# A state-space scan in chunks of 8 tokens and two halves of the groups instead of chunks of 4 and four quads, with its taps written through DRAM

## The chip, the cores and the metric

The kernel runs on one core of a Trainium2 chip. The core has five engines with a queue of instructions each: PE (TensorE) for matrix products, DVE (VectorE), ACT (ScalarE) and POOL (GpSimd) for elementwise work, and SP (SyncE), which here does nothing but issue the transfers (DMAs). The metric is the time of one execution in microseconds; the median of several runs counts.

## The reference

It is one decoder layer on 512 tokens of width 1024, in float32. A modulated RMS norm of x goes through one input projection, whose columns feed two groups of heads: a state-space mixer (S5) and a sparse attention. Both are gated, joined, projected and added to x. The change is in the state-space mixer. It has 32 groups of 16 channels, each with a complex diagonal state of 64 (`a_re`, `a_im`):

```python
lam_bar = jnp.exp(lam * dt)
b_bar = ((lam_bar - 1.0) / lam)[..., None] * b_mat
bu = jnp.einsum('gpc,bsgc->bsgp', b_bar, ug)
_, states = lax.associative_scan(_ssm_combine, (a_seq, bu), axis=1)   # s_t = lam_bar * s_(t-1) + bu_t
y = jnp.einsum('gcp,bsgp->bsgc', c_mat, states).real + d_skip * uf
z = jax.nn.gelu(y)
z = z * jax.nn.sigmoid(z @ w_glu + b_glu)
```

The attention scores each pair of tokens with an indexer, keeps the 128 best keys of each query, and takes a softmax over them with a bias that depends on the distance (`rel_bias`, by buckets).

## The kernel before

**Recording and order.** The kernel's functions don't issue instructions. They record them in `P`, stage by stage, with the engines that each may run on. `Plan.schedule` then simulates the five engines with the costs of `_cost`, and sets the order on every engine by the numbers of the tables STAGES (a start and a slope for each stage), SHIFT (an offset for a name in a stage), ONLY (the engines allowed), SLOTS (buffers of each pool) and KEEP. `_paired` says which instructions of DVE and POOL the planner lets wait for one another. `Plan.issue` puts the result out, so every instruction of the program has one line, L422. The order on an engine is fixed when the program is built; at run time an engine takes the next instruction as soon as what it needs is there, and what stands behind a waiting instruction waits too. All DMAs stand in SP's one queue.

**The work, in the order of its stages.** x0, x1: the norm of the two halves of x; x is transposed on PE (px). mod0 to mod4: the modulation's products (pm, pmt) and, as each piece of 128 channels of h comes (split into a high and a low part, hh and hl), the products of the index projection (pi), whose inputs are 640 columns of `in_w_in`. Every projection is three products for one (hh with wh, hl with wh, hh with wl), because the weight `wr` is split into `wh` and `wl` by ACT, DVE or POOL. Then come the values v0 and v1 (pv, pt), the index scores and the top keys (pr, acc, MAX8, MATCH_REPLACE8), the gates za, z2, z3 and the queries and keys qk0 to qk3 (all pp), the attention in four pairs of heads (pl, lg, ppt, po, at0 to at3), the gated linear unit of the state-space part (pgl, glu) and the output projection (pout).

**The state-space part.** `tables(q)` makes, for each quad q of 8 groups, what the scan needs: the weights W1 that take 4 tokens into the state (padded to 32 rows for the pairs of groups: padw, made by `cprod`, transposed by PE as ptw), W2 that takes the state back (w2, five powers of the decay), the taps Kt (pK, the direct way from inputs to outputs inside a chunk) and the block-triangular T, which is cleared by a memset on POOL and filled by four DMAs from kd, a copy of Kt in DRAM. `ssm_quad(q)` does the scan itself. The inputs u of one quad lie in U as 128 rows (4 tokens x 32) by 4 x 128 chunks. pd is W1 times U; DVE turns it by the phase (cos, sin), scans with the decay (TENSOR_TENSOR_SCAN) and turns it back (Xr, Xi); py is T times U plus W2 times Xr and Xi. Its result goes through a gelu and, through yd in DRAM, back to channel order (zt). U comes through DRAM too (ud).

**The bias.** `bias_rows` writes a row of biases for each of the 8 heads to bd in DRAM, and one DMA from DRAM to DRAM repeats it 128 times into bskew, from which each attention tile reads its skewed bias G.

Of the kernel before, what the change touches and what calls it, by code (L numbers as in the profile page):

```python
# [111 lines left out]
def _cost(eng, method, args, kw):  # L112
# [17 lines left out]
    if eng == "DVE":  # L130
# [7 lines left out]
        if method in ("tensor_copy", "tensor_scalar", "tensor_scalar_mul") and not ps:  # L138
            return 80 + 61 * aps + 0.521 * n
        return 69 + 61 * aps + 1.042 * n  # L140
# [18 lines left out]
def _paired(eng, method, args, kw):  # L159

    if eng == "POOL":
        return method not in ("memset", "iota")
# [10 lines left out]
    return n >= 2  # L173


class Plan:
# [73 lines left out]
    def schedule(self):  # L250
# [48 lines left out]
        while len(order) < len(ops):  # L299
# [68 lines left out]
            if e == "SP":  # L368
# [4 lines left out]
                dma = max(dma, hw + 500) + size / 305.0 * (2 if v.shape[-1] < 128 else 1)  # L373
                fin = dma + 900
# [50 lines left out]
class Eng:  # L425
# [18 lines left out]
SLOTS = {"t2": 65, "raw": 4, "ws": 8, "w2": 4, "psum": 8, "m8": 8}  # L444
BYTES = {"t2": 2048, "raw": 4096, "ws": 4096, "w2": 2560, "m8": 32}
KEEP = {"t2": 0, "raw": 15, "ws": 9, "w2": 0, "psum": 0, "m8": 0}
WINDOW = 506.5
# [7 lines left out]
    "const": (-753.2, 27.26), "warm": (-173.12, 802761090585146.2), "x0": (-752.23, 136.21), "x1": (-422.14, 15.05),  # L455
    "half0": (-64.92, 331.47), "half1": (108.73, 2.354074717163716e+16), "cond": (-674.9, 21.09),
    "cols": (-477.52, 211.29), "pars": (-269.91, 1.06), "mod0": (-469.03, 178.39), "mod1": (-148.91, 4.96),
    "mod2": (-149.72, 4.8), "mod3": (-159.94, 81.59), "mod4": (-64.92, 2.52), "idx2": (-240.13, 67.24),
    "idx": (66.28, 1.52), "rel": (-97.06, 84.25), "par": (123.19, 7.61), "lam": (-133.39, 1.1441577559218786e+16),
# [131 lines left out]
def record(P, a, out):  # L591
# [394 lines left out]
    def cprod(Xr, Xi, q, nd, nm, dst, neg):  # L986
# [8 lines left out]
        for e in range(2):  # L995
            G.memset(dst[e], 0.0)
# [564 lines left out]
```

## Time and profile before

| | |
|---|---|
| median of 3 runs | 358.12 us (356.9, 358.93, 358.12) |
| profiled execution | 355.87 us |
| its span, first to last instruction | 354.2 us |
| PE busy | 324.9 us, 92% |
| DVE busy | 289.4 us, 82% |
| ACT, POOL busy | 129.9 us, 110.5 us |
| PE's mean granted clock | 0.964 |

The span leaves out 1.67 us of the execution around the first and last instruction. Busy time says how long an engine had an instruction in it. An engine at 92% can still be the one that sets the end, and what matters then is what it waits for in the remaining 8%, and whether its products run at its full clock (1.0 is 2.4 GHz, and the lower level is half).

### The profile page before, as it was taken

Reading aid. Unit: us, or ns where it says so; the run is one execution under the profiler, and the core shown is the slowest. Engines: PE = TensorE matmul, PEld = TensorE weight load, DVE = VectorE, ACT = ScalarE, POOL = GpSimd, SP = SyncE. Lnnn points to the kernel's source line nnn. Section 1 sums busy time; section 2 is a strip of 40 time slices with the busy share of each in tenths; the row PEclk is TensorE's granted clock in tenths of the full one; section 3 lists DMA queues with packets and bytes.
Section 4 is the critical chain, followed back from the end, with each engine's and each line's share of the span. In section 5 each row is a group of like instructions: output and inputs, shape, how many; then the busy total and the mean of one; then the engine's idle time right before and its main releaser. Section 6 shows DMA issues by size and latency. Waiting matters only on the chain.

```text
span 354.2 us, 5839 instructions
## 1 busy us (share of the span) xinstructions
PE 324.9 (92%) x2022; PEld 265.4 (75%) x2023; DVE 289.4 (82%) x679; ACT 129.9 (37%) x264; POOL 110.5 (31%) x143
## 2 busy tenths in 40 slices
PE   5829969999995997999999998999999999999996
PEld 3717649788783886888888867877888777888785
DVE  5677994889999199999994999999999795896613
ACT  3423452117472116533431152332555884303000
POOL 3740227031974926531542600201800201100000
PEclk9879978999999699999999999999999999999999
DMA  7799775724264221623714483461380107266011
GB/s 224 221 307 348 139 227 160 214 62 118 52 192 144 82 62 49 187 64 116 207 34 119 127 237 104 138 210 40 93 269 28 59 3 268 89 216 230 30 61 60
DMA packets 57358, 49.50 MB, mean 140 GB/s; under 512 B 11224, under 2 KB 47400, under 8 KB 57328
## 3 DMA queue, kind: packets, MB, share of 16 engines
q1 hardware_dynamic: 57328, 49.13, 46.7%
q8 instruction: 16, 0.26, 0.3%
q14 instruction: 14, 0.11, 0.1%
HBM read 44.64 MB, written 6.05 MB: 143 GB/s over the span
## 4 chain that ended last, share of the span: by engine, by line
PE 67%; DVE 16%; DMA 10%; SPq 3%; issue 2%; ACT 1%; POOL 0%; DVEq 0%; POOLq 0%; ACTq 0%
PE pp L422 24%; PE pout L422 11%; PE pi L422 5%; PE pl L422 4%; DMA bskew<-bd 4%; PE pt L422 3%; PE py L422 3%; PE pgl L422 3%; PE po L422 3%; SPq L422 3%; PE ppt L422 2%; PE pv L422 2%; DVE stg L422 2%; PE pd L422 2%; DMA wa<-in_w_ada_dram 2%
## 5 line engine op out<-in xcount | busy, mean ns | idle before, releaser
L422 PE MATMUL pp<-hh,wh 128*128 128x512 f32 x152 | 61.5, 406 | 4.4 <-POOL wh L422 4.4
L422 PE MATMUL pp<-hl,wh 128*128 128x512 f32 x152 | 60.7, 400 | 0.0
L422 PE MATMUL pp<-hh,wl 128*128 128x512 f32 x152 | 60.2, 403 | 0.0
L422 POOL TENSOR_TENSOR wl<-wr,wh 128x1024 fp32r<-128x1024 f32 (+1 forms) x15 | 35.6, 2385 | 37.7 <-ACT wh L422 24.0
L422 ACT ACTIVATE wh<-wr 128x1024 fp32r<-128x1024 f32 (+1 forms) x27 | 25.9, 971 | 34.6 <-PE pout L422 20.5
L422 PEld LDWEIGHTS pp<-hh,wh 128*128 128x128 f32 x152 | 29.3, 193 | 10.4 <-POOL wh L422 4.8
L422 PEld LDWEIGHTS pp<-hl,wh 128*128 128x128 f32 x152 | 29.3, 193 | 5.7
L422 PEld LDWEIGHTS pp<-hh,wl 128*128 128x128 f32 x152 | 29.0, 191 | 6.0 <-issue 0.4
L422 DVE TENSOR_TENSOR wl<-wr,wh 128x1024 fp32r<-128x1024 f32 (+1 forms) x24 | 27.3, 1156 | 7.5 <-PE pi L422 4.6
L422 PE MATMUL pout<-wl,yh 128*128 128x512 f32 (+1 forms) x72 | 26.4, 367 | 0.4 <-DVE wl L422 0.4
L422 PE MATMUL pout<-wh,yl 128*128 128x512 f32 (+1 forms) x72 | 26.1, 366 | 0.0
L422 PE MATMUL pout<-wh,yh 128*128 128x512 f32 (+1 forms) x72 | 26.0, 370 | 0.1
L422 DVE MATCH_REPLACE8 work<-m,work 128x256 f32<-128x256 f32 (+2 forms) x45 | 24.1, 539 | 0.0
L422 DVE MAX8 m<-work 128x8 f32<-128x256 f32 (+2 forms) x45 | 23.2, 545 | 0.0
L422 ACT ACTIVATE lg<-lg,nm 128x256 f32<-128x256 f32 (+3 forms) x32 | 17.6, 552 | 4.1 <-DVE nm L422 4.1
L422 DVE TENSOR_TENSOR pout<-pout,gb 128x512 f32<-128x512 f32 (+1 forms) x9 | 5.7, 638 | 15.1 <-PE pout L422 15.0
L422 PE MATMUL pi<-hh,wh 128*128 128x384 f32 (+2 forms) x50 | 15.8, 361 | 1.6 <-DVE hh L422 1.6
L422 DVE CUSTOM_DVE_ANT_0 lg<-pl,G 128x256 f32<-128x256 f32 (+3 forms) x32 | 13.8, 485 | 3.4 <-PE pl L422 3.4
L422 POOL TENSOR_SCALAR wh<-wr 128x1024 fp32r<-128x1024 f32 x9 | 9.7, 1083 | 21.6 <-PE pp L422 13.2
L422 PE MATMUL pi<-hl,wh 128*128 128x384 f32 (+2 forms) x50 | 16.2, 338 | 0.0
L422 PE MATMUL pi<-hh,wl 128*128 128x384 f32 (+2 forms) x50 | 15.9, 339 | 0.0
L422 PEld LDWEIGHTS pout<-wl,yh 128*128 128x128 f32 x72 | 13.6, 189 | 2.8 <-DVE wl L422 0.6
(292 smaller groups left out, 792.2 us busy)
## 6 DMA issues: line engine op xcount, KB each, us to landing
wa<-in_w_ada_dram SPq DMA_DIRECT2D x32, 256.0 KB, 5.8
wr<-in_w_in_dram SPq DMA_DIRECT2D x13, 512.0 KB, 4.6
wr<-in_w_in_dram SPq DMA_DIRECT2D x24, 256.0 KB, 3.3
wr<-in_w_out_dram SPq DMA_DIRECT2D x8, 512.0 KB, 5.7
wag<-in_w_ada_dram SPq DMA_DIRECT2D x8, 512.0 KB, 5.0
x<-in_x_dram SPq DMA_DIRECT2D x8, 256.0 KB, 3.6
xr<-in_x_dram SPq DMA_DIRECT2D x8, 256.0 KB, 5.4
out_dram<-oo SPq DMA_DIRECT2D x7, 256.0 KB, 3.8
```

What stands on the lines that cost most here:

```text
L422: getattr(engines[eng], method)(*[val(a) for a in args], **{k: val(a) for k, a in kw.items()})
```

## The change

The scan works on 8 tokens a chunk, so a row of U holds 8 tokens x 16 channels and there are 64 chunks instead of 128. Instead of four quads there are two halves of the groups, each of two quads' tables: `ssm_half(r)` runs after tables 1 and 3. The two quads of a half lie in the upper and lower 64 partitions of the state, and share one chain of DVE instructions. Their pd products have 64 stationary columns each and are issued in pairs, side by side; the products with the states have 64 rows each and are paired too. The weights W1 and W2 have no zeros to be filled in any more. The taps with their zeros go to a DRAM tile zd, 256 x 240, and each T tile is read from it by 8 strided DMAs of 64 KB (before: 4 DMAs of 16 to 64 KB into a cleared tile). U is read by one DMA of 256 KB per quad. bskew is four tiles of two heads. Parameters are loaded in more and smaller pieces. Buffer counts change (t2 from 65 to 52, and a new pool tt of 6), the planner treats POOL's memsets as excluding DVE's paired operations, and gives DRAM writes a longer latency; and all numbers of the order are new, so that every engine's order differs. In the profile of the changed kernel the line of all instructions is L431.

```diff
 def _paired(eng, method, args, kw):
     if eng == "POOL":
-        return method not in ("memset", "iota")
+        return True
...
-SLOTS = {"t2": 65, "raw": 4, "ws": 8, "w2": 4, "psum": 8, "m8": 8}
+SLOTS = {"t2": 52, "tt": 6, "raw": 4, "ws": 8, "w2": 4, "psum": 8, "m8": 8}
...
-    "tab3": (287.71, 23.67), "u0": (42.98, 31.6), "u1": (57.28, 511.21), "ssm0": (304.54, 320.39),
+    "tab3": (-371.6824, 65.9471), "u0": (269.1514, 95.3904), "u1": (352.9992, 4.1434), "ssm0": (785.1089, 222.22),
...
-    Q = (128, 4, 128)
+    Q = (128, 8, 64)
...
-        for e in range(2):
-            G.memset(dst[e], 0.0)
...
-        Tt = t2(f"T{q}", shape=Q, parts=True)
-        G.memset(Tt, 0.0)
-        kd_ = P.tile("dram", f"kd{q}", [128, 128])
-        N.dma_start(kd_, Kt)
-        for jj in range(4):
-            N.dma_start(Tt[32 * jj:32 * jj + 32, :, (3 - jj) * 32:128],
-                        kd_[:, 0:(jj + 1) * 32].rearrange("(m c) x -> c m x", m=4))
+        N.dma_start(ZD[r][128 * (q % 2):128 * (q % 2) + 128], Kt)
+        if q % 2:
+            for h in range(2):
+                Tt = TT[2 * r + h] = P.tile("tt", f"T{2 * r + h}", [128, 8, 128], parts=True)
+                for i in range(8):
+                    N.dma_start(Tt[i::8], ZD[r].raw((16, 8, 128), lambda t, i=i, h=h: bass.AP(
+                        tensor=t.tensor, offset=t.offset + 16 * h * 240 + (7 - i) * 16,
+                        ap=[[240, 16], [32 * 240, 8], [1, 128]])))
...
-    def ssm_quad(q):
+    def ssm_half(r):
...
-            for m in range(4):
-                T.matmul(pd[:, m * 128:(m + 1) * 128], W1[q, e][:, m * 128:(m + 1) * 128], U[:, m, :],
-                         start=True, stop=True)
+            for m in range(8):
+                with P.together():
+                    for h in range(2):
+                        T.matmul(pd[64 * h:64 * h + 64, m * 64:(m + 1) * 64], W1[r][e][:, m, 64 * h:64 * h + 64],
+                                 Us[h][:, m, :], start=True, stop=True, skip_group_check=True)
...
+        for m in range(8):
+            o = slice(m * 64, m * 64 + 64)
+            for h in range(2):
+                T.matmul(pys[h][:, o], TT[2 * r + h][:, m], Us[h][:, m],
+                         start=(m == 0), stop=False, skip_group_check=True)
+        for m in range(8):
+            o = slice(m * 64, m * 64 + 64)
+            for e, x_ in enumerate((Xr, Xi)):
+                with P.together():
+                    for h in range(2):
+                        p_ = slice(64 * h, 64 * h + 64)
+                        T.matmul(pys[h][:, o], W2[2 * r + m // 4][e][p_, m % 4, 1:9].rearrange("p d c -> p (d c)"),
+                                 x_[p_, m], start=False, stop=(e == 1 and m == 7), skip_group_check=True)
...
-        N.dma_start(bskew.rearrange("h (p n) -> h p n", n=385)[:, :, 0:384],
-                    bd.raw((8, 128, 384), lambda t: bass.AP(tensor=t.tensor, offset=t.offset + 256,
-                                                            ap=[[640, 8], [0, 128], [1, 384]])))
+        for i in range(4):
+            bskew.append(P.tile("dram", f"bskew{i}", [2, 128 * 385]))
+            N.dma_start(bskew[i].rearrange("h (p n) -> h p n", n=385)[:, :, 0:384],
+                        bd.raw((2, 128, 384), lambda t, i=i: bass.AP(tensor=t.tensor, offset=t.offset + 1280 * i + 256,
+                                                                     ap=[[640, 2], [0, 128], [1, 384]])))
```

The order at three places. First, POOL in the norm of x, before (x is scaled by rstd; w, T, bb, padw, Xr and Xi are buffers of the tables):

```order
L422 TENSOR_SCALAR x_1_68<-x_1_68,rstd_40_201 128x512
L422 TENSOR_SCALAR x_4_74<-x_4_74,rstd_40_201 128x512
L422 MEMSET Xi_246 128x4
L422 MEMSET padw_53_249 128x512
L422 MEMSET Xr_253 128x4
L422 TENSOR_TENSOR wl_276<-wr_170,wh_259 128x640
L422 MEMSET w_11_65_305 128x640
L422 MEMSET T_70_327 128x512
L422 MEMSET w_01_73_341 128x640
L422 MEMSET bb_75_355 128x128
L422 MEMSET bb_77_362 128x128
L422 MEMSET padw_79_368 128x512
```

and with the change:

```order
L431 MEMSET bb_45_179 128x128
L431 MEMSET Kt_182 128x112
L431 MEMSET blk_115 64x1 x4
L431 TENSOR_SCALAR x_6_78<-x_6_78,rstd_56_226 128x512
L431 TENSOR_TENSOR wl_317<-wr_186,wh_298 128x640
L431 TENSOR_SCALAR x_12_90<-x_12_90,rstd_73_320 128x512
L431 TENSOR_SCALAR hf_485<-xT_65_278,Ac_105_462,Bc_102_456 128x256
L431 TENSOR_SCALAR wh_501<-wr_376 128x640
```

The clearing of padw, w and T that stood among and behind the scalings of x is gone, and what memsets there are stand ahead of them.

Second, the queue of transfers (SP) at the bias table, before:

```order
L422 DMA kd_330_1346<-Kt_1330 128x128
L422 DMA wr_338_1363<-in_w_in_dram 128x4x128 x2
L422 DMA bskew_1369<-bd_933 1024x1x384
L422 DMA T_97_433<-kd_327_1338 32x4x32
L422 DMA T_97_433<-kd_327_1338 32x4x64
L422 DMA T_97_433<-kd_327_1338 32x4x96
L422 DMA T_97_433<-kd_327_1338 32x4x128
L422 DMA T_70_327<-kd_330_1346 32x4x32
L422 DMA T_70_327<-kd_330_1346 32x4x64
L422 DMA T_70_327<-kd_330_1346 32x4x96
L422 DMA T_70_327<-kd_330_1346 32x4x128
L422 DMA wr_365_1495<-in_w_in_dram 128x4x128 x2
```

and with the change:

```order
L431 DMA ud_251_1050<-us_1042 128x512
L431 DMA bskew_253_1055<-bd_913 256x1x384
L431 DMA bskew_254_1057<-bd_913 256x1x384
L431 DMA bskew_256_1062<-bd_913 256x1x384
L431 DMA bskew_258_1067<-bd_913 256x1x384
L431 DMA G_259_1070<-bd_913 128x256
L431 DMA G_260_1074<-bd_913 128x256
L431 DMA U_1110<-ud_251_1050 128x8x64
L431 DMA wr_273_1127<-in_w_in_dram 128x4x256
L431 DMA wr_275_1143<-in_w_in_dram 128x4x256
```

The T loads that stood behind bskew, in front of the next weight (wr) and ud, are gone from there; four smaller transfers are followed by G, U and weights.

Third, PE at the last scan. Before, between the taps' products of one quad (py_2513) and those of the last (py_2565):

```order
L422 MATMUL py_2513<-Xi_566,w_13_493_2068 128x128
L422 MATMUL prt_2534<-ident_70,rp_1617 128x128 x4
L422 MATMUL pp_2492<-hh_187_734,wh_555_2376 128x512
L422 MATMUL pp_2492<-hl_190_748,wh_555_2376 128x512
L422 MATMUL pp_2492<-hh_187_734,wl_563_2408 128x512
L422 MATMUL pp_2492<-hh_185_726,wh_555_2376 128x512
L422 MATMUL pp_2492<-hl_197_775,wh_555_2376 128x512
L422 MATMUL pp_2492<-hh_185_726,wl_563_2408 128x512
```

and so on, twelve weight products pp in all, up to `py_2565<-U_1217,T_141_564`. With the change, behind the last pd product (pd_2735) of the second half to run:

```order
L431 MATMUL pd_2735<-U_1814,w_10_542_2556 64x64
L431 MATMUL pn_2766<-ident_86,nsq_2724 128x128 x4
L431 MATMUL psel_2773<-ident_86,blk_579_2713 128x128 x2
L431 MATMUL py_2798<-U_1814,T_586_2754 128x64 x8
L431 MATMUL prt_2815<-ident_86,rp_2150 128x128 x4
L431 MATMUL py_2821<-U_1110,T_592_2782 128x64 x8
L431 MATMUL pbx_2835<-rT_2823,sel_2826 128x512
L431 MATMUL pbx_2837<-rT_2823,sel_2826 128x512
L431 MATMUL pbx_2840<-rT_2823,sel_2826 128x512
L431 MATMUL pbx_2842<-rT_2823,sel_2826 128x512
L431 MATMUL py_2821<-Xr_2675,w_00_534_2513 128x64
L431 MATMUL py_2798<-Xr_2675,w_00_534_2513 128x64
```

Between the last pd and the first product with Xr stand transposes of the norm, the T products and four pbx, and no weight product.

## Rows read from the trace of the kernel before

**Rows 1.** The page: busy time, share and instructions of each engine.
```profile
PE 324.9 (92%) x2022; PEld 265.4 (75%) x2023; DVE 289.4 (82%) x679; ACT 129.9 (37%) x264; POOL 110.5 (31%) x143
```

**Rows 2.** Windows: span, busy us (instructions), PE's clock, DMA share, GB/s.
```profile
0.00:31.60 31.60, 19.87 (x186) 14.53 (x186) 20.31 (x63) 12.54 (x25) 14.05 (x54) 0.84 0.88 266
31.60:50.80 19.20, 16.07 (x123) 11.65 (x123) 17.70 (x76) 7.66 (x14) 5.36 (x2) 0.95 0.84 213
50.80:63.50 12.70, 12.68 (x59) 11.89 (x63) 7.87 (x20) 3.39 (x6) 6.41 (x8) 0.81 0.55 162
...
114.30:124.30 10.00, 10.00 (x42) 8.42 (x43) 2.68 (x7) 1.11 (x3) 9.54 (x11) 0.69 0.28 80
...
200.00:222.00 22.00, 19.89 (x139) 15.41 (x138) 20.82 (x41) 9.52 (x14) 1.92 (x1) 1.00 0.60 171
222.00:306.00 84.00, 83.29 (x609) 67.64 (x609) 74.66 (x189) 43.24 (x105) 18.79 (x14) 1.00 0.38 121
```

**Rows 3.** Chain that ended last, at the start: start us, us, what.
```profile
14.31 7.47 DVE stg L422
```

**Rows 4.** Timeline, 14 to 24 us: start us, us, engine, line, operation.
```profile
14.45 0.64 POOL L422 MEMSET w<- 128x640 f32 x1
14.66 0.19 ACT L422 ACTIVATION_READ_ACCUMULATOR junk<-x 128x1 f32 x1
...
21.69 0.15 POOL L422 MEMSET Xr<- 128x4 f32 x1
21.82 0.16 DVE L422 TENSOR_TENSOR ms<-ss 128x2 f32<-128x2 f32 x1
```

**Rows 5.** POOL's instructions by line and shape: count, busy us, mean ns.
```profile
L422 POOL MEMSET w<- 128x640 f32 x8 | 4.9, 636 | 4.8 <-PE py L422 4.8
```

**Rows 6.** Chain that ended last, 95 to 114 us.
```profile
95.97 12.84 DMA bskew<-bd
...
113.20 1.06 POOL wh L422
```

**Rows 7.** Timeline, 96 to 115 us, DMA queue and PE.
```profile
96.78 12.34 SPq L422 DMA_DIRECT2D T<-kd  x8
...
114.30 0.80 PE L422 MATMUL pp<-hh,wh 128*128 128x512 f32 x1 [4.35 <-POOL wh L422]
```

**Rows 8.** Chain that ended last, four runs of PE records.
```profile
122.23 1.79 PE pd L422 x16
...
218.31 2.92 PE py L422 x24
...
255.85 3.23 PE pt L422 x27
...
292.64 4.52 PE po L422 x80
```

**Rows 9.** Timeline, PE at 280 us.
```profile
280.44 0.72 PE L422 MATMUL pl<-qk,qk 64*128 64x128 f32 x8
```

**Rows 10.** DVE's instructions by line: count, busy us, mean ns.
```profile
L422 DVE TENSOR_TENSOR pd<-pd,cos 128x512 f32<-128x512 f32 x16 | 10.6, 689 | 0.0
...
L422 DVE TENSOR_TENSOR_SCAN pd<-dec,pd 128x512 f32<-128x512 f32 x8 | 9.4, 1206 | 0.0
...
L422 DVE CUSTOM_DVE_ANT_0 lg<-pl,G 128x256 f32<-128x256 f32 (+3 forms) x32 | 13.8, 485 | 3.4 <-PE pl L422 3.4
```

**Rows 11.** Chain that ended last, 212 to 219 us.
```profile
212.96 1.92 DMA kd<-Kt
...
216.21 1.91 DMA T<-kd
```

**Rows 12.** Timeline, 214 to 219 us, DMA queue and PE.
```profile
214.90 1.74 SPq L422 DMA_DIRECT2D T<-kd  x4
...
218.31 0.46 PE L422 MATMUL py<-U,T 128*128 128x128 f32 x2 [1.26 <-DMA T<-kd]
```

More of the change, by code (lines that the diff above doesn't have):

```diff
@@ L139, in _cost @@
             return 80 + 61 * aps + 0.521 * n
+        if out.base.name in ("ya", "ys") and len(out.shape) > 2:
+            return 69 + 1.94 * n
         return 69 + 61 * aps + 1.042 * n
@@ L173, in _paired, with _dram @@
     return n >= 2
+def _dram(way):
+    vs = [isinstance(v, View) and v.base.pool == "dram" for v in way[2][:2]]
+    return vs[0], all(vs)
 class Plan:
@@ L553 @@
-    "bias:pb": -124.7, "bias:brow": 18.6, "bias:brow2": -6.1, "bias:bd": 26.1, "bias:bskew": -26.1,
[18 rows of a table removed]
+    "const:ident": 85.268, "const:identb": 22.023, "const:zero": 40.092, "warm:pi0": -41.874, "warm:pi1": 32.785,
[4 rows of a table added]
+    "cols:psm": 3.997, "cols:mcol": -1.031, "pars:ld2": -40.116, "pars:stg": -15.44, "pars:pst": 6.806,
[19 rows of a table added]
+    "par:blk": -49.228, "par:blk4": 9.999, "par:psel": -35.233, "par:sel": 99.294, "par:hpi": -22.367,
+    "par:nrow": -43.414, "par:ones_n": -1.15, "par:ones_f": -9.762, "lam:st1": 81.265, "lam:st2": -20.414,
[5 rows of a table added]
@@ new lines @@
+    "bc:c_re_l": -6.972, "bc:cd": 9.033, "bc:pcm": 3.882, "bc:c_re_t": 2.04, "bc:c_im_t": 0.998,
[29 rows of a table added]
+    "norm:pn": 24.679, "norm:rq_s": 23.609, "norm:rqk": 67.517, "norm:rq_t": 1.602, "norm:rp": 27.307,
+    "norm:prt": -1.164, "norm:rT": -8.38, "bias:rbp": -10.194, "bias:oh": -9.493, "bias:oh_r": 4.246,
+    "bias:pb": 2.666, "bias:brow": 4.148, "bias:brow2": 30.786, "bias:bd": -47.516, "bias:bskew0": 31.287,
[16 rows of a table added]
+    "gate:wag": -1.883, "gate:pmg": 9.221, "gate:grow_h": 62.367, "gate:pgb": 1.642, "gate:gb0": 1.092,
@@ L572 @@
+    "gate:gb1": 23.929, "out0:wl2": -0.966, "out0:xr": -73.998, "out0:oo": 80.526, "out0:out": 3.708,
+    "out1:wr2": 0.123, "out1:wh2": 7.903, "out1:wl2": -3.805, "out1:xr": 14.489, "out1:pout": -0.182,
+    "out1:oo": 0.061, "out1:out": -5.254,
 }
@@ L833, in record @@
     stage("par")
-    eye = small("eye", [128, 32], parts=True)
-    for r in range(4):
-        p_ = slice(32 * r, 32 * r + 32)
-        V.tensor_copy(eye[p_], ident[p_, p_])
+    eye4, eye2, eye = small("eye4", [128, 64]), small("eye2", [128, 32]), small("eye", [128, 16])
+    V.tensor_add(eye4, ident[:, 0:64], ident[:, 64:128])
+    V.tensor_add(eye2, eye4[:, 0:32], eye4[:, 32:64])
+    V.tensor_add(eye, eye2[:, 0:16], eye2[:, 16:32])
     causal = small("causal", [128, 128])
@@ L922, in record @@
     cmul(Pr[:, 2], Pi[:, 2], Pr[:, 1], Pi[:, 1], Pr[:, 1], Pi[:, 1], (128, 16))
[L923 to L925 removed]
+    for d in (2, 4):
+        up = lambda P_: P_[:, d:d + 1].to_broadcast([128, d, 16])
+        cmul(Pr[:, d + 1:2 * d + 1], Pi[:, d + 1:2 * d + 1], Pr[:, 1:d + 1], Pi[:, 1:d + 1], up(Pr), up(Pi), (128, d, 16))
+    nPr = st((128, 9, 16))
     V.tensor_scalar(nPr, Pr, -1.0, None, op0=ALU.mult)
[L927 to L929 removed]
+    Pr7, Pi7 = (small(nm, [128, 8, 16], parts=True) for nm in ("Pr7", "Pi7"))
+    for i in range(8):
+        hi(Pr7[:, i], Pr[:, 7 - i])
+        hi(Pi7[:, i], Pi[:, 7 - i])
+    rho8 = st()
+    V.tensor_mul(rho8, rho, rho)
+    V.tensor_mul(rho8, rho8, rho8)
+    V.tensor_mul(rho8, rho8, rho8)
     den, nr, cfr, cfi, tq = st(), st(), st(), st(), st()
@@ L1292, in norms @@
         evac(rT, prt)
-    bd, bskew = P.tile("dram", "bd", [8, 640], parts=True), P.tile("dram", "bskew", [8, 128 * 385])
+    bd, bskew = P.tile("dram", "bd", [8, 640], parts=True), []
     def bias_rows():
```

227 lines of the change are left out of this document (115 added, 112 removed), and 200 rows, old and new, of tables (ONLY, SHIFT, STAGES).

## The prediction

> **What bounds the kernel now.** I read the page first, then the windows, then the chain of work that ended last, and last the timeline at the places where the chain leaves TensorE. The page has PE at work for 324.9 of 354.2 us and DVE for 289.4 [rows 1]. So a DVE instruction that goes is worth something only where PE stands still for it, and PE's own time and its idle time have to be counted apart. I cut the windows where PE stands or runs slowly [rows 2]. It idles 11.7 us up to 31.6, where the first index projection (pi) starts, 3.1 us from there to 50.8, and 2.1 us between 200 and 222. From 114.3 to 124.3 it never idles, but its granted clock is 0.69; from 50.8 to 63.5 the clock is 0.81. From 222 to 306, the attention, PE is busy for 83.3 of 84 us and DVE for 74.7. Elsewhere there is little to win but PE's own work.
>
> At three places the kernel stands for something that the change touches. First, the chain has a DVE copy of a 16x128 tile (stg) that takes 7.47 us [rows 3]. The timeline shows what lies beside it: ACT has the last square sum of x at 14.85; POOL begins a run of memsets at 14.45 and ends it at 21.84; the copy ends at 21.78, and the norm's next DVE operation (ms) starts at 21.82 [rows 4]. I read the copy as held by the whole run. Second, the transfer that writes bskew lasts 12.84 us, and POOL's split of a weight behind it starts only at 113.20 [rows 6]. In that stretch the queue needs 12.34 us for eight issues of T tiles, and PE starts again at 114.30, after 4.35 idle us [rows 7]. Third, PE waits 1.26 us for the taps T [rows 12].
>
> **The change part by part.** *Start.* The 8 memsets of w take 4.9 us of POOL [rows 5]; with the tables' zero padding they go, those of padw and T too. In the order no run of memsets is left behind POOL's first scalings of x; the next one there comes forty rows later. If nothing holds the copy, the norm can go on at 14.9 instead of 21.82: 6.9 us. More can come back behind it, since PE's 3.1 idle us up to 50.8 and its slow clock from 50.8 to 63.5 (0.81 over 12.7 us: 2.4 us of work) are of the same wait for the modulation. Transfers set the limit: their engines are 0.88 and 0.84 busy up to 50.8 and 0.55 in the next 12.7 us [rows 2], so what comes after 63.5 can't move up by more than those 12.7, and the new kernel has more small parameter loads in front. I take -10, between the copy alone (-7) and -12; below, -0.6 is the bound.
>
> That bound is one of a page. The Trainium skill, page "SBUF — State Buffer", section "Who interferes with whom", says that DVE and GpSimd share a pair of ports under an exclusive lock, held for one whole instruction, so that the second to come waits for the other's instruction. By that, the copy would have waited for one memset (0.64 us in the row of rows 4), and the sum would be +4.5. The trace has the copy end with the last memset of the run and not with the first, and I go by the trace.
>
> *The bias table.* The transfer of bskew becomes four, of two heads each, and on the queue no T load stands behind them: there come G tiles, U and the weights of za, which PE takes only after the products of v0 and of the index scores, far later. The stall of 4.35 us goes. The 10 us behind it, at 0.69, hold 6.9 us of work at full clock, so 3.1 more go: -7.4. Bounds: 0, if the queue is held there by these four in the same way, and -7.5.
>
> *The scan's products.* A quad has 16 records of pd in 1.79 us and 24 of py in 2.92 (two records to a product) [rows 8]; four quads make 18.8 us. After the change there are 64 half-width products of pd in pairs (128 records), 32 of T (64 records) and 64 row halves on the states (128 records), all with 64 moving columns where there were 128. The trace has none with 64. Nearest to pd are the 80 records of po, column halves in pairs, in 4.52 us [rows 8], 0.057 each: 7.3. For T I take the price of the full products now, 0.117: 7.5. Nearest to the row halves are 8 records of pl with 64 rows in 0.72 us [rows 9], 0.09 each: 11.5. Together 26.3, or +7.5. If half the columns cost half, it is 13.2 (-5.6); if nothing pairs and columns don't count, 320 records at 0.117 are 37.4 (+18.6). I take +4: the prices are those of 128 columns, and some of the halving should show, most on T.
>
> *Vector work.* Two of four scan chains go: eight products of about 0.69 us, four sums like them and two scans of 1.206 each [rows 10], some 10.7 us a chain, 21 together. I count nothing for it, because PE is busy beside DVE with the projections; where that cover ends, at the last scan, the next term has it. The bound is -3. The wider tables, the powers and the small copies of Pr7 and Pi7 go the other way on DVE and ACT and are hidden alike.
>
> *The last half.* Now the taps of the last two quads and their scan end together. The order shows that behind the last pd there are left only the transposes pn, psel and prt, the taps' products and four pbx before PE needs the states; twelve weight products (pp) stood between the last two scans' products before. The taps need a write of Kt (1.92 to land), sixteen issues of 0.44 (four take 1.74), and 1.91 to land [rows 11, 12]: 10.8 us. The states need the chain of 10.7 and some 2.4 of norm operations among it: 13 us. PE has in that time 3.7 us of T products (half of the 64 records at 0.117) and about 2 of the rest: 7.3 idle, less the 2.1 of before [rows 2]: +5. Bounds: 0, if attention fills it, and +12, if half of the sixteen issues take the 1.54 us that each of eight took beside bskew [rows 7] (15.8 + 3.8 - 5.7 - 2.1 = 11.8).
>
> *Attention.* The 96 products of v1 (pt; 27 records take 3.23 us [rows 8], so 11.5 us) move out of this stretch to an earlier one. PE then has 71.8 us where DVE has 74.7 [rows 2], of which the logits alone take 32 x 0.485 [rows 10]. So about +2; bounds 0 (if DVE's work moves too) and +8 (if the gate's products can't fill either).
>
> *Clock.* The stall of 4.35 us was followed by 3.1 lost to the clock. A gap of 7 us can cost the same: +1.5, between 0 and 3.
>
> Sum: -10 - 7.4 + 4 + 5 + 2 + 1.5 = -4.9 on the profiled execution's 355.87 us: 351.0. The median of the runs is 2.25 above that execution, so **353**.
>
> **The rivals.** (1) The half tiles don't pair: +18.6 instead of +4 gives a sum of +9.7, some 368 in the median. For it: no row has products of 64 columns; against it: po, which pairs. It turns the sign from +9 on. (2) The copy was held by something other than the run of memsets, which the change leaves: -0.6 in place of -10, a sum of +4.5, 363. For it: the transfers are nearly full there; against it: the two ends that meet. Halfway, with transfers that take back 5 us, it is 358, no change. (3) The last half's gap is at its bound with the whole slow clock: +7 and +1.5, a sum of +3.6, 362. For it: the slow issues beside bskew; against it: they stood behind a 1.5 MB transfer, and here 120 KB are written. (4) Attention's products cover the gap, and columns count: no +5, no +1.5 and nothing in place of +4, a sum of -15.4, 343. For it: the attention has products of its own that wait for neither; against it: the order, which puts few of them ahead.
>
> **How the numbers follow.** This kernel's measurement can't tell changes under 0.5% from none. Chances: the forecast with its surroundings (348 to 358) 0.56, (1) 0.06, (2) 0.09 and its half-way case 0.10, (3) 0.07, (4) 0.12. The range, 343 to 363, leaves out (1) and what lies beyond (2) and (4). Faster (under 356.3) is most of the forecast's case, 0.50, and (4): 0.62. Slower (over 359.9) is (1), (2) and (3): 0.22. The rest is 0.16.
>
> **What would show it.** Start: the 16x128 copy under 1 us, and the first pi near 22; if the copy is short and the first pi is after 28, transfers bind. Queue: no idle of over 2 us of PE before the first za product, and a clock near 1.0 there. Products: pd and py together 19 to 26 us. Last half: 5 to 9 us of PE idle in front of the first product with Xr, put down to DVE or to T. The prediction is wrong if the copy stays long, if the gap is over 10 us, or if the row halves take over 0.1 us a record.

## The result, and the profile after

The changed kernel is slower: 370.85 us in the median (369.24 to 372.02, 4 runs) against 358.23 us (356.90 to 358.93), a ratio of 1.035 with a 95% interval of 1.030 to 1.040. The forecast was 353 us, and its range ended at 363. The profiled execution took 369.24 us, with a span of 367.5 us: 13.3 us more than the 354.2 of before. Runs of one kernel differ by up to some 3%, and the profiled runs of e6, e9 and e11 below are among the longest of theirs, so only distances inside a stretch are read from them.

The page of the changed kernel: busy time, share and instructions of each engine, and PE's clock in 40 slices of 9.2 us (tenths).

```profile
PE 338.9 (92%) x2183; PEld 274.2 (75%) x2183; DVE 278.7 (76%) x669; ACT 124.2 (34%) x253; POOL 116.3 (32%) x118
PEclk9699999999979999999998999985569999999999
```

DVE has 10.7 us less than in [rows 1], PE 14 us more. The second row says where to look: the clock is down in three slices together at two thirds of the span, where it was full before. I cut the windows there, and around the two places that the prediction spoke of (span, busy us and instructions of PE, PEld, DVE, ACT and POOL, PE's clock, DMA share, GB/s).

```profile
0.00:26.65 26.65, 20.84 (x189) 15.58 (x189) 16.00 (x62) 12.23 (x26) 8.65 (x39) 0.87 0.73 225
26.65:60.00 33.35, 32.80 (x224) 26.78 (x224) 31.04 (x126) 13.49 (x24) 4.68 (x4) 1.00 0.95 294
60.00:100.00 40.00, 37.07 (x210) 33.44 (x209) 36.62 (x64) 22.43 (x51) 12.66 (x7) 0.96 0.32 84
66.00:90.00 24.00, 21.07 (x127) 19.32 (x126) 22.56 (x38) 9.96 (x28) 11.11 (x7) 0.93 0.14 46
100.00:120.00 20.00, 14.48 (x54) 11.24 (x53) 13.49 (x26) 3.76 (x5) 16.18 (x12) 0.83 0.49 149
120.00:240.00 120.00, 118.09 (x787) 97.09 (x786) 92.81 (x203) 27.53 (x43) 48.67 (x40) 0.99 0.41 114
240.00:246.00 6.00, 0.92 (x10) 0.64 (x6) 6.00 (x12) 2.17 (x3) 1.27 (x1) 0.91 0.29 63
246.00:272.00 26.00, 23.23 (x131) 18.37 (x132) 14.41 (x41) 8.28 (x18) 0.00 (x0) 0.50 0.17 40
```

The same two stretches of the kernel before, which the prediction did not need:

```profile
60.00:100.00 40.00, 38.65 (x257) 32.77 (x255) 36.08 (x81) 17.69 (x47) 18.05 (x20) 1.00 0.40 112
100.00:120.00 20.00, 15.65 (x62) 12.20 (x61) 15.87 (x34) 8.02 (x18) 12.49 (x19) 0.84 0.53 152
```

From a window one gets the time that PE lost in it: what it idled, plus its busy time times one minus the clock. Before, the first 63.5 us lost 21.3 by [rows 2]; now the first 60 lose 5.8 + 2.7 + 0.6 = 9.1. **The start won 12.2 us.** Then it is given back: 60 to 100 loses 4.4 where it lost 1.4 (+3.1), 100 to 120 loses 8.0 where it lost 6.9 (+1.1). And 240 to 272 loses 7.9 idle and 0.1 + 11.6 to the clock, 19.6, while the attention of before had lost 0.7 in 84 us [rows 2]. From 120 to 240 there is about 1 less. Together that is some +10; the remaining 3 of the 13.3 are more work at full clock. This is a count of PE's time; how much of it the kernel gets back when a loss goes is for the experiments to say.

### The profile page after: what moved, and what is told of

Same layout as the page of the kernel before. It is cut to its first block, busy times and chain, and to the rows that moved or that the text cites. A ratio compares the mean times of both kernels' runs of the same rounds, so it can differ in the third digit from the quotient of the medians.

```text
span 367.5 us, 6158 instructions
## 1 busy us (share of the span) xinstructions
PE 338.9 (92%) x2183; PEld 274.2 (75%) x2183; DVE 278.7 (76%) x669; ACT 124.2 (34%) x253; POOL 116.3 (32%) x118
## 4 chain that ended last, share of the span: by engine, by line
PE 68%; DVE 11%; SPq 8%; DMA 7%; ACT 2%; issue 2%; POOL 1%; DVEq 0%; ACTq 0%; POOLq 0%
PE pp L431 26%; PE pout L431 12%; SPq L431 8%; PE pl L431 5%; PE py L431 5%; PE pi L431 4%; PE pgl L431 3%; PE po L431 3%; PE ppt L431 3%; DVE st L431 2%; DMA wr<-in_w_in_dram 2%; PE pr L431 2%; DMA x<-in_x_dram 2%; DVE pd L431 2%; DMA wa<-in_w_ada_dram 1%
## 5 line engine op out<-in xcount | busy, mean ns | idle before, releaser
L431 PE MATMUL pp<-hh,wh 128*128 128x512 f32 x152 | 60.9, 404 | 2.9 <-POOL wh L431 2.9
L431 PE MATMUL pp<-hh,wl 128*128 128x512 f32 x152 | 60.4, 405 | 2.7 <-POOL wl L431 2.7
L431 PE MATMUL pp<-hl,wh 128*128 128x512 f32 x152 | 60.8, 402 | 0.0
L431 POOL TENSOR_TENSOR wl<-wr,wh 128x1024 fp32r<-128x1024 f32 (+1 forms) x20 | 45.5, 2283 | 45.5 <-ACT wh L431 27.0
L431 PEld LDWEIGHTS pp<-hh,wl 128*128 128x128 f32 x152 | 29.5, 194 | 10.0 <-POOL wl L431 3.7
L431 PEld LDWEIGHTS pp<-hh,wh 128*128 128x128 f32 x152 | 29.6, 194 | 9.2 <-POOL wh L431 3.3
L431 PEld LDWEIGHTS pp<-hl,wh 128*128 128x128 f32 x152 | 29.3, 193 | 6.0
L431 ACT ACTIVATE wh<-wr 128x1024 fp32r<-128x1024 f32 (+1 forms) x21 | 19.8, 964 | 25.2 <-DMA wr<-in_w_in_dram 10.1
L431 PE MATMUL pout<-wl,yh 128*128 128x512 f32 (+1 forms) x72 | 26.5, 368 | 0.0
L431 PE MATMUL pout<-wh,yh 128*128 128x512 f32 (+1 forms) x72 | 26.1, 371 | 0.0
L431 PE MATMUL pout<-wh,yl 128*128 128x512 f32 (+1 forms) x72 | 25.9, 367 | 0.0
L431 DVE TENSOR_TENSOR wl<-wr,wh 128x1024 fp32r<-128x1024 f32 (+1 forms) x19 | 22.3, 1189 | 3.6 <-PE pp L431 2.0
L431 DVE MATCH_REPLACE8 work<-m,work 128x256 f32<-128x256 f32 (+2 forms) x45 | 24.3, 549 | 0.0
L431 DVE MAX8 m<-work 128x8 f32<-128x256 f32 (+2 forms) x45 | 23.2, 554 | 0.0
L431 ACT ACTIVATE lg<-lg,nm 128x128 f32<-128x128 f32 (+3 forms) x32 | 17.7, 554 | 7.7 <-DVE nm L431 7.6
L431 PE MATMUL py<-U,T 128*128 128x64 f32 x64 | 11.3, 350 | 9.5 <-DMA T<-zd 9.5
L431 POOL TENSOR_SCALAR wh<-wr 128x1024 fp32r<-128x1024 f32 (+1 forms) x11 | 11.8, 1078 | 25.6 <-DMA wr<-in_w_in_dram 19.1
L431 DVE CUSTOM_DVE_ANT_0 lg<-pl,G 128x128 f32<-128x128 f32 (+3 forms) x32 | 14.5, 484 | 6.7 <-PE pl L431 6.0
L431 PEld LDWEIGHTS py<-U,T 128*128 128x128 f32 x64 | 10.7, 261 | 11.0 <-issue 11.0
L431 POOL TENSOR_SCALAR yh<-ya 128x512 fp32r<-128x512 f32 x3 | 1.9, 627 | 49.5 <-DVE ya L431 49.5
L431 PE MATMUL pl<-qk,qk 64*128 64x128 f32 (+3 forms) x64 | 15.4, 533 | 0.0
```

The source lines that it names most:

```text
L431: getattr(engines[eng], method)(*[val(a) for a in args], **{k: val(a) for k, a in kw.items()})
```

## The experiments

All are edits of one of the two kernels; the order of the rest stays as it is. Times are medians; the kernel before was run beside them on the same chip, and had 356.98 us for the first four kernels, 355.58 for the next four, 357.11 for e9 and e10, 353.75 for the last two, where its single runs lay between 347.8 and 358.8. Kernels of one chip are therefore compared with one another first: e1 to e4, e5 to e8, e9 and e10, e11 and e12. The changed kernel's 370.85 is from another set, and e1, which came out like it (370.14), stands for it beside e2 and e3. In the code, ... marks what is left out.

**e1: the gap of the last half filled.** 100 products of a bf16 identity go to py's bank before the first T product of the last half.

```diff
+    order[k:k] = [(fill, ("PE", "matmul", (py[:, 0:128], idb, idb), dict(start=True, stop=True, skip_group_check=True)))] * 100
```

> The changed kernel with 100 products of a bf16 identity with itself put on TensorE in front of the first product with the taps of the last half, where it stood idle for 7.16 us. They write a bank that the next product overwrites; nothing else is changed. Theory (the gap lowers the granted clock, and the thin products behind it then run at half speed until 272 us): the clock from 250 to 270 is 1.00 instead of 0.50, the taps and states arrive as before, and the kernel is 10 to 12 us faster than the changed one, some 359 to 361. Rival (products of 64 columns and half the rows get the low clock by themselves, gap or not): the clock stays near 0.5 from 252 on and the time stays at 370. Second rival (the low clock costs nothing because ACT and DVE bound the attention): the clock is 1.00 and the time falls by less than 3 us.

It took 370.14 us, as the changed kernel, where 359 to 361 was expected. The timeline of its PE (start us, us, what, and in brackets the idle time before and what ended it):

```profile
241.51 5.75 PE L431 MATMUL py<-identb 128*128 128x128 bf16 x100
248.39 1.97 PE L431 MATMUL py<-U,T 128*128 128x64 f32 x16 [1.13 <-DMA T<-zd]
253.53 3.65 PE L431 MATMUL py<-U,T 128*128 128x64 f32 x16 [2.73 <-DMA T<-zd]
258.26 0.69 PE L431 MATMUL py<-Xr,w 64*128 64x64 f32 x4
```

The first tap products now ran at full clock (1.97 for 16 instead of 3.64) and left a longer wait for the second T tile. Its windows give a clock of 1.00 from 240 to 252 and 0.51 from 252 to 272. Nothing was won, because the path went through the second tile all the time: PE stood 2.73 us in front of it, and the clock was lost there a second time.

**e2: the four bias transfers with the 128 rows outermost**, the same bytes.

```diff
-            N.dma_start(bskew[i].rearrange("h (p n) -> h p n", n=385)[:, :, 0:384],
...
-                                                                     ap=[[640, 2], [0, 128], [1, 384]])))
+            N.dma_start(bskew[i].rearrange("h (p n) -> p h n", n=385)[:, :, 0:384],
...
+                                                                     ap=[[0, 128], [640, 2], [1, 384]])))
```

> The changed kernel with the same four transfers of the bias table, but with the 128 rows as the outermost dimension of each instead of its two heads. Theory (a transfer is spread over the DMA engines by its outermost dimension, so each of the four ran on two engines of sixteen, DMA share 0.13 to 0.15, and kept the queue for 30 us): the share between 62 and 75 us is over 0.5, the four and the G tile behind them leave the queue within 12 us instead of 30, the weight of za is there before PE needs it, PE's 5.5 idle us between 100 and 108 go, and the time falls by 5 to 9 us. Rival (the volume of 1.5 MB from DRAM to DRAM is slow on any number of engines): the queue is held as long as before and the time changes by less than 2 us.

361.43 us, 9.4 less than the changed kernel and 8.7 less than e1; ratio to before 1.010 (1.005 to 1.016). The queue, first in the changed kernel:

```profile
62.63 19.96 SPq L431 DMA_DIRECT2D bskew<-bd  x4
82.70 9.60 SPq L431 DMA_DIRECT2D G<-bd  x2
...
92.91 6.24 SPq L431 DMA_DIRECT2D wr<-in_w_in_dram  x2
```

and in this one:

```profile
62.69 2.58 SPq L431 DMA_DIRECT2D bskew<-bd  x4
65.37 3.89 SPq L431 DMA_DIRECT2D G<-bd  x2
...
70.62 3.49 SPq L431 DMA_DIRECT2D wr<-in_w_in_dram  x2
```

In the changed kernel the queue is held for 30 us, and the transfer engines are 0.14 busy meanwhile (66 to 90, at 46 GB/s), which is about two of 16. With the rows outermost the share is 0.75, 0.92 and 1.00 in the three slices of 4 us from 64 (the last two hold the weights too), the weights' issue begins 22 us earlier, and from 80 to 180 PE doesn't idle at all. The Trainium skill says this on its page "DMA: Bandwidth & Descriptors", section "Rules for kernel authors": an outermost dimension under 16 confines a transfer to at most as many engines. The traces agree: two heads gave 0.14.

**e8: the four transfers made one**, the heads outermost as before, now eight.

```diff
+    big = P.tile("dram", "bskew", [8, 128 * 385])
...
+        tensor=t.tensor, offset=t.offset + 256, ap=[[640, 8], [0, 128], [1, 384]])))
```

> The changed kernel with one part undone: one transfer of the bias table with its eight heads as the outermost dimension, as before, at the place of the first of the four; all else in the changed order. If the outermost dimension sets the number of DMA engines (two heads: share 0.13; 128 rows: the queue was free after some 9 us), eight heads give a share near 0.5 and hold the queue some 13 us, the weight of za lands before 95 and the 5.5 idle us of TensorE are gone or under 2: 361 to 366. If splitting in four is not what made it slow: no change, 370.

359.61 us (358.45 to 360.52), ratio to before 1.015 (1.007 to 1.022). Its queue:

```profile
63.81 0.73 SPq L431 DMA_DIRECT2D bskew<-bd  x1
64.59 3.35 SPq L431 DMA_DIRECT2D G<-bd  x2
...
68.56 7.21 SPq L431 DMA_DIRECT2D wr<-in_w_in_dram  x2
```

The transfer leaves the queue at 64.5, and the share from 64 to 68 is 0.57 (0.13 in the changed kernel, 0.75 in e2). So it was the split into pieces of two heads that cost about 10 us by the medians (some 7 by the ratios to the kernel before, since this is another chip), and nothing else about the bias table.

**e3: the last half's taps early.** Its 16 T loads are issued ahead, from the other half's zd (wrong taps in two of the four quads, the same bytes).

```diff
+    Ts = [(op, (w[0], w[1], (w[2][0], View(zd1, w[2][1].arr, w[2][1].chain, w[2][1].dtype)), w[3]))
+          for op, w in order if isT(op, w)]
...
+    order[k:k] = Ts
```

> The changed kernel with the 16 loads of the last half's taps taken from the DRAM tile of the other half and issued some 7 us earlier, behind zt, so that they wait for no Kt (the output is then computed with the wrong taps in two of four quads). Theory (the late taps are what holds TensorE from 241 to 258): its products with the taps start by 242, it waits for Xr until 249 and Xi until 250 at most, the first product with the states comes at 250 instead of 258, and the time falls by 8 us for the gap, and by up to 10 more if the clock doesn't fall: 353 to 363. Rival (the scan on DVE ends at 250 anyway and the gap is only moved in front of the states): the clock falls all the same, and the time falls by 8 at most, 362 to 366.

366.11 us, 4.7 less than the changed kernel and 4.0 less than e1, just past the 362 to 366 of the rival. Its PE timeline:

```profile
243.31 2.91 PE L431 MATMUL py<-U,T 128*128 128x64 f32 x16 [2.44 <-DMA T<-zd]
248.23 1.09 PE L431 MATMUL prt<-ident,rp 128*128 128x128 f32 x4 [2.00 <-DVE rp L431]
249.11 3.52 PE L431 MATMUL py<-U,T 128*128 128x64 f32 x16
253.71 0.69 PE L431 MATMUL py<-Xr,w 64*128 64x64 f32 x4
```

The states' products begin 4.3 us earlier than in the changed kernel (258.00). But two waits are left, 2.44 us still for T (the sixteen issues begin at 235.18 and take 11.16 us) and 2.00 for the norm's vector work (rp), and the clock is 0.50 from 244 to 268 all the same. The gap is not that of the taps alone.

**e5: e2, with both waits for taps filled** by identity products into the bank of pn: 120 before T1's products, 50 before T0's.

```diff
+    order[at("T0"):at("T0")] = [fill(pn)] * 50
+    order[at("T1"):at("T1")] = [fill(pn)] * 120
```

> The kernel with the row-wise bias transfers, and filling products (bf16 identity, into a bank that is free again) at both waits of the last half: 120 in front of the first tap products, 50 in front of the second. With the first wait alone filled, two waits of 1.1 and 2.7 us were left and the clock still fell to 0.50. Theory (any standing of TensorE there lowers the clock; the thin products alone don't): with no idle time of over 0.7 us between 230 and 250 the clock stays at 1.00 through the products with the states, they take some 7.5 us instead of 15, and the kernel is 8 to 11 us faster than the one with the row-wise transfers alone, 351 to 354. Rival (64-column and half-row products lower the clock by themselves): the clock falls to 0.5 in the state products though there was no idle time, and the time stays at 360 to 363.

357.56 us (356.26 to 359.93, 10 runs). Beside it on that chip e6, which has no fill, took 361.32 (below). Two windows:

```profile
232.00:252.00 20.00, 19.16 (x282) 18.18 (x280) 13.42 (x33) 3.21 (x7) 0.00 (x0) 1.00 0.23 55
252.00:260.00 8.00, 6.99 (x25) 3.09 (x25) 6.52 (x22) 5.99 (x15) 0.00 (x0) 0.59 0.20 49
```

Work that computes nothing makes the kernel faster by some 4 us: the tap products take 1.97 instead of 3.65, four products with the states 0.39 instead of 0.64. That is the theory's clock with half of its gain of 8 to 11. The second tap products begin at 244.58, and at 244.37 in e2 at half clock: up to there the low clock cost next to nothing, because the second tile wasn't there sooner. Behind the states, at 253.5, PE waits 0.90 us for yg, and from 252 to 260 the clock is 0.59 on average.

**e6: e2, with T0's eight loads on ACT's queue**, and **e7: e6 with the fill** (120 and 20).

```diff
+    T0 = [(op, ("ACT",) + w[1:]) for op, w in filter(isT, order)]
+    order[k:k] = T0
```

> The kernel with the row-wise bias transfers, and the eight loads of the second tap tile of the last half issued by ScalarE's queue, behind its square root of the norm, beside the eight of SyncE. Theory (sixteen issues of 0.64 us in one queue are what the second tap products and with them the states wait for): the second tap products start right behind the first and the transposes, 3 to 5 us earlier than with one queue, and the kernel is 3 to 5 us faster than 361. Rival (the tap's path is bound by the landing of zd and by the transfers themselves, which share the engines): the loads take twice as long side by side, and the time changes by less than 1.5 us.

> Both: row-wise bias transfers, the second tap tile on ScalarE's queue, and filling products at the waits (120 and 20). If the two effects add, the states' products start 3 to 5 us earlier and run at full clock: 346 to 350, below both the kernel before and the changed one. If the clock falls without idle time, 356 to 359.

e6 took 361.32 us, as e2 did on another chip (ratios to before 1.018 and 1.010, with intervals that overlap). The second tile is there in time now, without a wait, but PE is behind: at half clock the 32 tap products, prt and pbx take from 244.56 to 253.45, 8.9 us, where e2 needs 9.9 with its wait of 0.64. e7 took 356.35 us (353.43 to 358.74), ratio to before 1.003 (0.998 to 1.008). So no gain of a second queue shows at the low clock; with the fill, e7 needs 30 products fewer than e5 and is 1.2 us shorter. The 346 to 350 expected if the two effects add didn't come.

**e11: e7 with the wait of 0.9 us filled too**, the last pbx issued six times more. **e12: e2, both waits left, and 120 identity products behind the last tap product**, where the clock is at 0.50.

```diff
+    order[last:last] = [order[last]] * 6
...
+    order[k:k] = [(fill, ("PE", "matmul", (pbx[:, 0:128], idb, idb), dict(start=True, stop=True, skip_group_check=True)))] * 120
```

> The kernel with the rows outermost, T0's loads on ACT's queue and both fills, in which also the last pbx product in front of the first mask product is issued six more times (the same product again, so the result is as before), so that the wait of 0.9 us for yg at some 254.9 is filled with 1.3 us of products. Theory that the waits of PE, short ones too, lower the clock: the clock stays at 1.0 through 256 to 260 (it was 0.57 there), 1.7 us of full-clock work come back, less 0.4 of products beyond the wait: about 355. Rival, the thin products before them lower it: the clock of that stretch stays near 0.57 and the time is 356 to 357.

> The kernel with the rows outermost, with both waits for the taps as they are (7.2 and 0.6 us), and 120 dense 128x128 bf16 products of the identity put behind the last tap product, in front of the first pbx of that stretch. The clock is 0.50 when they begin. Theory that it rises with dense work, and that the thin products alone don't bring it back: it is at 1.0 when the fill ends, and the products with the states, 0.64 per four before, take 0.39; the fill costs 7 to 13 us and the faster products give back 5 to 7: 361 to 369. Rival, it stays low for the same stretch whatever PE does: the clock is 0.50 through the fill and into the state products, which still take 0.64 per four, and the time is 368 to 375.

e11 took 357.05 us, with runs from 351.12 to 362.31 that can't tell one microsecond. Its windows can:

```profile
254.00:256.00 2.00, 2.00 (x20) 1.69 (x18) 2.00 (x8) 1.97 (x4) 0.00 (x0) 1.00 0.03 8
256.00:258.00 2.00, 2.00 (x11) 0.83 (x9) 2.00 (x7) 1.98 (x3) 0.00 (x0) 0.84 0.13 33
258.00:260.00 2.00, 2.00 (x8) 0.71 (x6) 1.50 (x6) 1.62 (x8) 0.00 (x0) 0.50 0.28 67
260.00:262.00 2.00, 2.00 (x11) 1.12 (x10) 1.40 (x5) 1.22 (x7) 0.00 (x0) 0.81 0.29 71
```

PE never stands still from 248 to 262, and the clock falls all the same, behind the products with the states and ten pbx of 32 rows. That is the rival's case: in this run no wait was needed for it. It is one run, of 358.08 us with a mean clock of 0.971; the shortest had 351.12 and 0.993, and whether the clock fell there too isn't on record. e12 (one run, 363.71 us) shows the other direction:

```profile
244.00:246.00 2.00, 2.00 (x12) 2.00 (x12) 0.00 (x0) 0.00 (x0) 0.00 (x0) 0.50 0.00 0
246.00:248.00 2.00, 2.00 (x19) 2.00 (x20) 0.00 (x0) 0.00 (x0) 0.00 (x0) 0.50 0.00 0
248.00:250.00 2.00, 2.00 (x24) 2.00 (x22) 0.00 (x0) 0.00 (x0) 0.00 (x0) 0.55 0.00 0
250.00:252.00 2.00, 2.00 (x40) 2.00 (x38) 0.00 (x0) 0.00 (x0) 0.00 (x0) 1.00 0.00 0
```

The fill begins at 246.20 and the clock is full from 250 on; the products with the states behind it take 0.39 for four. In e2, the same products follow the same waits without a fill:

```profile
232.00:240.00 8.00, 0.77 (x4) 0.80 (x4) 8.00 (x18) 0.26 (x1) 0.00 (x0) 0.76 0.36 83
240.00:262.00 22.00, 21.36 (x127) 17.14 (x126) 11.01 (x33) 7.95 (x16) 0.00 (x0) 0.50 0.13 30
```

The clock is 0.50 from 240 to 262, with PE busy for 21.4 of these 22 us. So the end of the waits didn't bring the clock back, nor did the 21.4 us of work behind them; in e12 it rose within the fill. Which property of the fill counts was not tried. The first fall, though, came inside a wait: in e2 the clock is 0.54 from 236 to 238 and 0.50 from 238, and the first tap product starts at 239.23; in the changed kernel it is 0.50 from 246 to 248, where PE has nothing to do.

**e4: the kernel before, with the copy of stg on ACT** instead of DVE. Does the run of memsets hold it?

```diff
+    k = next(i for i, (op, w) in enumerate(order) if w[1] == "tensor_copy" and w[2][0].base.name == "stg")
+    order[k] = (order[k][0], ("ACT", "activation", order[k][1][2] + (AF.Copy,), {}))
```

> The kernel before with its one copy of the 16x128 tile run by ScalarE instead of VectorE, all else in the same order. Theory (the copy was held by POOL's whole run of memsets): the norm's operation at 21.82 starts before 16, the first index projection before 27 instead of 31.6, and the kernel before is 5 to 10 us faster, 348 to 353. Rival (the page's lock of one instruction, and something else makes that stretch slow): the next VectorE operation is as late, the time stays within 1 us of 358. Second rival (the transfers bind): the norm is early but the first index projection comes after 29, and the gain is under 4 us.

356.93 us beside 356.98: no change, where 5 to 10 us were expected. The timeline of DVE and ACT:

```profile
15.11 0.31 ACT L422 ACTIVATE stg<-ld 16x128 f32<-16x128 f32 x1
15.12 0.16 DVE L422 TENSOR_TENSOR ms<-ss 128x2 f32<-128x2 f32 x1 [1.80 <-ACT junk L422]
15.31 4.92 DVE L422 TENSOR_SCALAR ms<-ms 128x2 f32<-128x2 f32 x1
```

The copy is done in 0.31 us, and the hold moves on: ms of 128x2 elements takes 4.92 us and ends at 20.23, while POOL's memsets go on to 21.9. So the hold lasts through many memsets, but here not to the last of them, as the copy's had seemed to. The first pi came at 29.31, 2.3 us earlier than before, and the time didn't follow.

**e9: the kernel before, with the wide memsets earlier**, in POOL's idle time at the start, the small ones behind the norm. **e10: e9 with one bskew transfer, rows outermost.**

```diff
+    big = [x for x in ms if x[0].writes[0].name[:2] in ("w2", "T0", "T1", "T2", "pa")][:12]
...
+    order[k:k] = big
...
+    order[k:k] = rest
...
-        N.dma_start(bskew.rearrange("h (p n) -> h p n", n=385)[:, :, 0:384],
...
-                                                            ap=[[640, 8], [0, 128], [1, 384]])))
+        N.dma_start(bskew.rearrange("h (p n) -> p h n", n=385)[:, :, 0:384],
...
+                                                            ap=[[0, 128], [640, 8], [1, 384]])))
```

> The kernel before with its POOL memsets moved and nothing else: twelve of the wide ones (padw, w, T) into POOL's idle time from 3.8 to 10.2 us, the small ones and one T behind the first scaled half of h. With the copy alone on ScalarE the hold went to the next operation of its kind, a TENSOR_SCALAR of 128x2 that took 4.92 us. Theory (a run of memsets on POOL holds VectorE's one-input operations until it ends): no VectorE operation of a small tile takes over 1 us between 10 and 20 us, the norm of the second half of x ends by 17, the first index projection comes at 24 to 27 instead of 31.6, and the kernel is 5 to 8 us faster than before. Rival (the transfers bind from there on): the first index projection is early but the next ones wait for weights, and the gain is under 2 us.

> The kernel before with the memsets moved and its one bias transfer with the 128 rows as the outermost dimension instead of the eight heads. With eight heads it lasted 12.84 us, at a share of 0.5 to 0.7. Theory: on all sixteen engines it lasts 7 to 9 us, the T loads behind it leave the queue 4 to 6 us earlier, the wait of 4.35 us for the weight and the low clock behind it go or shrink, and the kernel is another 3 to 7 us faster: 343 to 348. Rival (the T loads behind it are slow by themselves, or the shared engines delay the weights as much): under 2 us of change.

The lines on bskew are e10's alone. e9 took 352.29 us (347.83 to 354.63), ratio 0.989 (0.972 to 1.007): not settled. The copy takes 0.35 us there, and the first pi comes at 26.67. e10 took 348.70 us (347.01 to 349.91), ratio **0.983 (0.971 to 0.994)**: faster than both kernels, though whether by 2% than the kernel before is open. Its distance to e9 lies within the runs' spread. Of its queue and PE:

```profile
90.75 0.66 SPq L422 DMA_DIRECT2D bskew<-bd  x1
91.50 10.97 SPq L422 DMA_DIRECT2D T<-kd  x8
...
107.72 0.80 PE L422 MATMUL pp<-hh,wh 128*128 128x512 f32 x1 [2.98 <-POOL wh L422]
```

The bias transfer's issue is over early (0.66 us), but in the chain of work that ended last the transfer itself lasts 11.40 us from 90.75 (12.84 before), not the 7 to 9 expected, and the eight T loads behind it still take 10.97 us to issue (12.34 before), so PE's wait shrinks only from 4.35 to 2.98. In the kernel before, the order of the transfer's dimensions was not the whole reason of that wait; the rival, slow T loads or shared engines, stands.

## Why the prediction was wrong, step by step

The timeline and chain of the changed kernel carry the points below.

```profile
13.76 0.22 DVE L431 COPY stg<-ld 16x128 f32<-16x128 f32 x1
...
103.85 0.50 PE L431 MATMUL pp<-hh,wh 128*128 128x512 f32 x1 [2.85 <-POOL wh L431]
...
107.47 0.80 PE L431 MATMUL pp<-hh,wl 128*128 128x512 f32 x1 [2.66 <-POOL wl L431]
...
241.07 10.19 SPq L431 DMA_DIRECT2D T<-zd  x16
...
248.08 3.64 PE L431 MATMUL py<-U,T 128*128 128x64 f32 x16 [7.16 <-DMA T<-zd]
...
253.27 3.65 PE L431 MATMUL py<-U,T 128*128 128x64 f32 x16 [0.69 <-DMA T<-zd]
```

```profile
171.87 2.04 PE pd L431 x64
...
194.94 1.97 PE py L431 x16
...
217.75 3.72 PE py L431 x64
...
237.46 3.56 DMA zd<-Kt
```

**Start, -10: right** (-12.2 by the windows). The copy takes 0.22 us where it took 7.47 [rows 3], and the first pi starts at 26.65 instead of 31.60: in the chain a transfer of wa, 4.78 us from 20.78, stands in front of it, as the prediction allowed for. One hold is left that nobody forecast: a DVE operation of 128x2 (rs_t) takes 1.31 us from 14.85 instead of 0.16, and ends with POOL's split of a weight beside it (14.60 to 16.13). About 3 of the 12.2 comes back by 100: PE waits 2.93 us at 80.51, in front of a table's transposes, for one DVE product (bw). That the memsets held the copy is borne out by e9, where the same copy takes 0.35 us once they are moved, and by e4. The Trainium skill, "SBUF — State Buffer", section "Who interferes with whom", lists copies and tensor_scalar among the operations that can take the port pair shared with GpSimd, and says that tensor_tensor contends only with GpSimd's reads. The traces agree: in e4, beside memsets, ms by TENSOR_TENSOR took 0.16 and the TENSOR_SCALAR behind it 4.92. The page's lock of one instruction is not what these rows show: the hold lasts through several memsets.

**Bias table, -7.4: wrong, the first of the two steps that failed.** "The stall of 4.35 us goes", because what is queued behind is needed "far later". It is needed at 103.85, and its issue starts only at 92.91, behind 30 us of bskew and G. PE stands for 2.85 + 2.66 us, where it stood for 4.35, and the clock is 0.83 from 100 to 120: the stall is as large as before and has changed its name. I had asked what stands behind the transfers and not how fast pieces of two heads move. The bound that I gave, 0, was where it came out (+1.1); e2 took 9.4 us back with the order of two dimensions.

**Scan products, +4: too high.** 64 records of pd take 2.04 us (0.032 each, not 0.057), 64 with the states 3.72 (0.058, not 0.09), 32 of T 1.97 + 1.90 (0.121, as with 128 columns [rows 8]; the halving of columns gave nothing on them). For two halves: 4.1 + 7.7 + 7.4 = 19.2 us against 18.8, so +0.4 at the full clock. Rivals (1) and (2) are out by this and the start. Of the 3 us of more work, 2.7 are thus not the scan's. 2.0 of them are the norm's sums psq, which the forecast didn't have: before, 16 records in one row took 1.94 us (at 204.78); now two lots of eight take 1.91 and 2.05 (at 174.71 and 236.40). The rest, 0.7, is not put down to any product.

**Vector work, 0: not tested by itself.** Two chains of 10.7 us went, and DVE has only 10.7 less, so its other work took about half of it back.

**Last half, +5: right in place and size.** The idle time is 7.9 us between 240 and 272, less 2.1: +5.8. The way to it was harder than forecast: the write of zd took 3.56 us to land instead of 1.92, the sixteen issues 0.64 each instead of 0.44, T 2.26; and e3, with the taps read ahead, keeps 4.4 us of waits, 2.0 of them for DVE.

**Clock, +1.5: wrong, the second step that failed.** PE lost 11.7 us of its time to it. I had carried over the 3.1 that the stall of 4.35 cost in the kernel before [rows 2, 7], where the weight products pp follow it and the clock averaged 0.69 over 10 us. That a wait of 7 us brings the clock down held: it was at 0.50 before the first tap product. How long it stays down did not: here the tap products, pbx and the products with the states follow, and the clock stayed at 0.50 for 26 us. e2 and e12 show that it didn't come back in the 22 us behind the waits, and did within the identity products of e12; e11 shows, in one run, a fall behind them without a wait. So rival (3) named the right place, and what was missing was its price: with +5.8 and +11.7 in place of +5 and +1.5, +1.1 for -7.4, +0.4 for +4, -12.2 + 3.1 for -10 and nothing for the +2, the sum is 355.87 + 9.9; with the 2.7 of other work it is 368.5, beside 369.24. The 11.7 is PE's time, not what the kernel would win: with the waits filled, e5 and e7 win 3.8 and 5.0 us on e6.

**Attention, +2: not seen.** DVE's work fell by 10.7 us, and from 272 to 360 PE idles 0.3 of 88 us at full clock. The products that moved out of this stretch were not missed there.

**Open.** Whether the two-half scan can be had without the gap: e7 fills it with work that computes nothing and ends level with the kernel before. Weight products in that place, and fewer loads per T tile, were not tried.

## What to carry to other kernels

When a transfer is cut into pieces, look at its outermost dimension first: two entries there gave 46 GB/s and held the queue for 30 us, 128 rows let it go after 6.6. Price a gap in TensorE's work with the products that come behind it: the stall before the weight products cost 0.7 of its length again in clock (3.1 on 4.35), the idle time among the products of the scan 1.5 times its length (11.7 on 7.9). Then ask how much of that lies on the path: filling the waits won 4 to 5 us. And look at what stands in GpSimd's queue beside a short vector chain: moving the memsets (e9, not settled by itself) together with a turned access pattern (e10, 1.7% faster than before) did more than the rebuilt scan.

## What the runs showed of the hardware that was not expected

- The bias transfer with two, eight or 128 entries outermost (changed kernel, e8, e2): DMA share 0.13, 0.57 and 0.75 from 64 to 68 us, and SP's queue held for 30, 4.1 and 6.6 us by it and the G tiles behind it.
- A DVE instruction of 128x2 elements took 4.92 us, one of 16x128 took 7.47, beside a run of GpSimd memsets of 0.1 to 0.6 us each; a two-input one among them took 0.16 (e4 and the kernel before).
- The clock fell to 0.50 while TensorE was busy without a break (e11, 256 to 260, one run), stayed there for 22 us with TensorE busy for 21.4 of them (e2), and rose from 0.50 to 1.00 within the 120 identity products of e12.
- Sixty-four products with 64 stationary and 64 moving columns, issued in pairs, took 2.04 us (0.032 each); sixteen records with 128 stationary and 64 moving columns took 1.97, no less than with 128 moving ones (24 in 2.92 before).
- Eight of the norm's products psq (32 stationary columns) took 2.05 us in a row by themselves, sixteen in one row 1.94.
